# Linear attention on one core: two of its seven pairwise levels multiplied in narrow column pieces

## The chip, the cores and the metric

The kernel runs on one NeuronCore of a Trainium2 chip. The metric is the device time of one execution in microseconds (us). Engines are named as in the profile: PE is the matmul engine and PEld its weight loads, DVE, ACT and POOL are the vector, scalar and general engines, SP issues most DMAs.

## The reference

One layer of a decoder step in float32: a prompt of 2048 tokens and 8 single decode tokens, width 1024. After a norm and one projection, half of the heads do sliding-window attention (window 128) and half do gated linear attention (4 heads, keys of 64, values of 128). Then come an output projection and a SwiGLU block of width 2816. The part that the change touches is the linear attention:

```python
def gla_chunked(q, k, v, log_a, s0):   # S_t = diag(a_t) S_{t-1} + k_t^T v_t, o_t = q_t S_t
    b = jnp.cumsum(ac, axis=2)
    o_inter = jnp.einsum('nhtd,nhdv->nhtv', qc * jnp.exp(b), S)
    decay = jnp.exp(jnp.where(causal, b[t] - b[s], -inf))
    scores = jnp.einsum('nhtd,nhsd,nhtsd->nhts', qc, kc, decay)
    o = o_inter + jnp.einsum('nhts,nhsv->nhtv', scores, vc)
```

## The kernel before

The program has three stages: projection and window attention (to about 427 us), linear attention (about 427 to 720 us), and the output projection with the SwiGLU block (the rest, a Strassen scheme of F32R matmuls). It is written with the Tile framework. The last lines of the file build it with `schedule_with_timeline_sim=True`: a scheduler orders each engine's instructions when the program is built, by dependencies and by durations that it estimates. What an engine runs is therefore not the order of the source, and work of neighbouring loop passes is interleaved.

The linear attention takes two chunks of 128 tokens at a time: `gla_b(pp)` for pp = 0 to 7, with `front_b(pp + 1)` (projections of the next pair, tiles `ps_qk`, `ps_v`, `ps_g`) after each. Inside `gla_b` the scores of a chunk are put together from seven levels, H = 64, 32, 16, 8, 4, 2, 1 (line 53 names them `LEVELS`). At level H a chunk falls into blocks of 2H tokens, and the queries of the upper half of each block meet the keys of its lower half. For each level:

- DVE forms differences of cumulated gates (`E`, L799), ACT takes the absolute value and the exponential (L800, L801).
- POOL writes decayed queries into one of three `bd` tiles (L813, two instructions); `bd[:, :, g]` holds two heads' 64 queries each, 128 columns. DVE multiplies the keys into `E` (L814).
- PE multiplies `E` and `bd` in float32 for the four pairs g = 2a + c of head pair a and chunk c (L817 and L818). All 128 tokens of a chunk stand as weights, so all 128 partitions of `ps_l` are written, though only the 64 lower-half tokens are wanted. The profile shows each float32 matmul as two records, hence 8 records a level.
- For H = 64 and 32 ACT copies the wanted rows out of PSUM into the score tile `AT` (L820 to L824, one copy and two copies). For the five smaller levels DVE copies under a mask (L828).

`ps_l` has two PSUM banks (pool `b_lv`). When all levels are done, `AT` is multiplied with the values (`po`, L867) and the state is updated: `pst` (L875) is a float32 matmul with 64 weight columns, whose results lie in partitions 0 to 63 and 64 to 127 in turn. Other float32 matmuls of the block are `ps_d` (L836), with two moving columns.

Of the kernel before, what the change touches and what calls it, by code (L numbers as in the profile page):

```python
# [20 lines left out]
P = 128  # L21
# [30 lines left out]
def hymba_kernel(ctx: ExitStack, tc: tile.TileContext, I, O, X=None, phases=3):  # L52
    nc = tc.nc
# [538 lines left out]
    with ExitStack() as ph:  # L592
# [69 lines left out]
        for i in range(2):  # L662
            AT = pc.tile([P, 4, 2, P], F32, name=f"AT{i}")
# [7 lines left out]
        for i in range(3):  # L671
            bd = bdp.tile([P, 2, 4, 64], F32, name=f"bd{i}")
# [98 lines left out]
        def split_wo(i, behind):  # L771


            if raw_wo:
                wr, dh, k0 = raw_wo.pop()
                hl = wop.tile([P, 2, 2, 512], F32R, tag="hl", name="wohl")
                with tc.issue_after(behind.ins):
                    split(hl[:, 0], hl[:, 1], wr.rearrange("p (k n) -> p k n", k=2))
                nc.sync.dma_start(wo_d[dh][:, :, k0:k0 + 2], hl.bitcast(F32))
            if i < 8:  # L780
                dh, k0 = i // 4, 2 * (i % 4)
                wr = wop.tile([P, 1024], F32, tag="wr", name="wro")
                for dst, src in load_wo(wr, k0, dh):
                    nc.sync.dma_start(dst, src)
                raw_wo.append((wr, dh, k0))

        def gla_b(pp):
            qT, kTt, Bt, vs, rs = live.pop(pp)

            AT = ATs[pp % 2]  # L790
            q2 = qT[:, :, 0:256].rearrange("p a (c t) -> p a c t", c=2)
            k2 = kTt[:, :, 0:256]
            for li, H in enumerate(LEVELS):
                J = 64 // H

                E = wl.tile([P, 2, 256], F32, tag="E", name="E", bufs=4)
                Bv = Bt.rearrange("p a (n t) -> p (a n) t", t=2 * H)
                Ev = E.rearrange("p a (n t) -> p (a n) t", t=2 * H)
                nc.vector.tensor_tensor(Ev, Bv, Bv[:, :, H - 1:H].to_broadcast([P, 4 * J, 2 * H]), ALU.subtract)  # L799
                nc.scalar.activation(E, E, AF.Abs)  # L800
                grown = nc.scalar.activation(E, E, AF.Exp, scale=-1.0 / 16)  # L801

                if li in (1, 5) and 2 <= 2 * pp + li // 5 <= 10:
                    split_wo(2 * pp + li // 5 - 2, grown)
                bd = bds[nbd[0] % 3]
                nbd[0] += 1
                qv = qT[:, :, 0:256].rearrange("p a (n two o) -> p a n two o", two=2, o=H)
                kv = kTt[:, :, 0:256].rearrange("p a (n two o) -> p a n two o", two=2, o=H)
                E5 = E.rearrange("p a (n two o) -> p a n two o", two=2, o=H)
                bv = bd.rearrange("p h (a c) (j o) -> p h a (c j) o", a=2, o=H)  # L810
                for h in range(2):
                    rows = slice(64 * h, 64 * h + 64)
                    nc.gpsimd.tensor_tensor(bv[rows, h], E5[rows, :, :, 1], qv[rows, :, :, 1], ALU.mult)  # L813
                nc.vector.tensor_tensor(E5[:, :, :, 0], E5[:, :, :, 0], kv[:, :, :, 0], ALU.mult)  # L814
                ps = lvp.tile([P, 512], F32, tag="lv", name="ps_l")
                Ef = E.rearrange("p a t -> p (a t)")
                for g in range(4):  # L817
                    nc.tensor.matmul(ps[:, g * P:(g + 1) * P], Ef[:, g * P:(g + 1) * P],  # L818
                                     bd[:, :, g], start=True, stop=True)
                if H >= 32:  # L820
                    for j in range(J):
                        rows = slice(2 * H * j, 2 * H * j + H)
                        nc.scalar.copy(AT[rows].rearrange("p g h t -> p (g h) t")[:, :, 2 * H * j + H:2 * H * j + 2 * H],
                                       ps[rows].rearrange("p (g t) -> p g t", t=64)[:, :, H * j:H * j + H])  # L824
                else:
                    av = AT.rearrange("p g h (j two o) -> p (g h) j two o", two=2, o=H)[:, :, :, 1]
                    mk = lmask[:, li * 64:(li + 1) * 64].rearrange("p (j o) -> p j o", o=H).unsqueeze(1)
                    nc.vector.copy_predicated(av, mk.to_broadcast([P, 8, J, H]),  # L828
                                              ps.rearrange("p (g j o) -> p g j o", g=8, o=H))
# [3 lines left out]
            ps = aux.tile([P, 512], F32, tag="aux", name="ps_d")  # L833
# [17 lines left out]
            ps = aux.tile([P, 512], F32, tag="aux", name="ps_kd")  # L851
# [5 lines left out]
            for c in range(2):  # L857
# [4 lines left out]
                for p in range(2):  # L862
                    g = 2 * p + c
                    last = p == 1
                    for h in range(2):
                        hc = slice((2 * p + h) * P, (2 * p + h + 1) * P)
                        nc.tensor.matmul(po[:, hc], AT[:, g, h, :], v[:, hc], start=(p == 0 and h == 0),  # L867
                                         stop=(last and h == 1 and b == 0), skip_group_check=True)
                    if b > 0:
                        nc.tensor.matmul(po[:, p * 256:(p + 1) * 256], eBf[:, g * P:(g + 1) * P], Sbd[:, p, :],  # L870
                                         start=False, stop=last, skip_group_check=True)

                    for h in range(2):
                        rows = slice(64 * h, 64 * h + 64)
                        nc.tensor.matmul(pst[rows, p * P:(p + 1) * P], kdN[:, g, rows], v[:, (2 * p + h) * P:(2 * p + h + 1) * P],  # L875
                                         start=True, stop=True)
                for p in range(2):
                    g = 2 * p + c
                    for h in range(2):
                        rows = slice(64 * h, 64 * h + 64)  # L880
# [3 lines left out]
                for hh in range(4):  # L884
                    p, h = hh // 2, hh % 2
# [13 lines left out]
                ps = aux.tile([P, 512], F32, tag="aux", name="ps_m")  # L899
# [57 lines left out]
        for pp in range(NB // 2):  # L957
            gla_b(pp)
            next(dec, None)
            if pp + 1 < NB // 2:  # L960
                front_b(pp + 1)
# [487 lines left out]
```

## Time and profile before

| what | value |
|---|---|
| runs, median (lowest to highest of 3) | 2265.45 us (2263.92 to 2266.01) |
| the profiled execution, its own time | 2265.43 us |
| span of that execution | 2263.7 us |
| granted PE clock, mean | 0.989 |
| matmul records of L818 | 448 |
| copies of L823 | 24 |

The profiled execution's time is its span and 1.7 us around it. Busy time and shares are counted inside the span. A matmul record's duration includes the pipeline behind it, so the rate of a group is read from the starts of its neighbours.

### The profile page before, as it was taken

The page shows a single profiled execution, that of the slowest core. Times are in us where ns is not written, and L with a number is a line of the kernel's source. Part 1 is how long each engine was busy: PE and PEld are TensorE (multiplying, and loading weights), DVE is VectorE, ACT ScalarE, POOL GpSimd, SP SyncE. Part 2 cuts the span into 40 slices and gives each one's busy share as a digit, 9 for nine tenths or more (in the row PEclk, how much of TensorE's full clock was granted, in tenths as well). Part 3 has the DMA queues.
Part 4 walks back from the last instruction along what each step waited for, and adds up shares of the span by engine and source line. Part 5 has one row for each costly group of instructions (what it writes and reads, how often), then busy time and mean ns, then how long its engine had stood idle before and what let it go on. Part 6 is the DMA issues. An engine that isn't in the chain of part 4 may idle for free.

```text
span 2263.7 us, 34888 instructions
## 1 busy us (share of the span) xinstructions
PE 2201.3 (97%) x12697; PEld 1903.6 (84%) x12697; DVE 1566.6 (69%) x3076; ACT 1006.7 (44%) x2259; POOL 624.7 (28%) x706
## 2 busy tenths in 40 slices
PE   8999998999998999999999999999999899999997
PEld 6888887888887788688888889999999878787886
DVE  6787888677765667776667666676766665757487
ACT  6766777465654334433323233333333334434342
POOL 2443434465664233211111111110111122222222
PEclk9999999999999999999999999999999999999999
DMA  7323334445515998933333375233332477878776
GB/s 235 119 75 108 111 106 159 116 150 172 168 49 217 330 317 275 350 112 95 110 98 94 116 253 203 85 117 89 103 99 87 148 195 176 202 168 230 166 209 233
DMA packets 211992, 364.75 MB, mean 161 GB/s; under 512 B 15683, under 2 KB 129116, under 8 KB 208732
## 3 DMA queue, kind: packets, MB, share of 16 engines
q1 hardware_dynamic: 174764, 259.05, 34.9%
q0 software_dynamic: 37056, 103.47, 18.0%
q8 instruction: 100, 1.64, 0.3%
q14 instruction: 72, 0.59, 0.1%
HBM read 211.24 MB, written 152.29 MB: 161 GB/s over the span
## 4 chain that ended last, share of the span: by engine, by line
PE 69%; issue 17%; POOL 6%; DVE 4%; DMA 2%; ACT 1%; SPq 0%; POOLq 0%; DVEq 0%; ACTq 0%
PE ps_b L108 6%; PE ps_b L107 6%; PE ps_b L109 6%; PE ps_c L108 4%; PE ps_c L107 4%; PE ps_c L109 4%; POOL h_d L1380 4%; PE ps_a L108 4%; PE ps_a L107 4%; PE ps_a L109 4%; PE ps_d L107 3%; PE ps_d L109 3%; PE ps_d L108 3%; PE ps_wo L107 2%; PE ps_wo L109 2%
## 5 line engine op out<-in xcount | busy, mean ns | idle before, releaser
L109 PE MATMUL ps_b<-z,whl 128*128 128x258 f32 (+1 forms) x792 | 253.4, 320 | 2.1 <-DVE whl L96 2.1
L107 PE MATMUL ps_b<-z,whl 128*128 128x258 f32 (+1 forms) x792 | 254.1, 321 | 1.2 <-ACT whl L95 1.2
L108 PE MATMUL ps_b<-z,whl 128*128 128x258 f32 (+1 forms) x792 | 254.3, 321 | 0.0
L95 ACT CAST dm<-mr 128x384 fp32r<-128x384 f32 (+1 forms) x224 | 108.3, 488 | 188.3 <-PE ps_b L109 100.8
L108 PE MATMUL ps_a<-z,whl 128*128 128x258 f32 (+1 forms) x528 | 169.2, 320 | 0.0
L108 PE MATMUL ps_c<-z,whl 128*128 128x258 f32 (+1 forms) x528 | 169.1, 320 | 0.0
L109 PE MATMUL ps_a<-z,whl 128*128 128x258 f32 (+1 forms) x528 | 168.9, 320 | 0.0
L109 PE MATMUL ps_c<-z,whl 128*128 128x258 f32 (+1 forms) x528 | 168.9, 320 | 0.0
L107 PE MATMUL ps_a<-z,whl 128*128 128x258 f32 (+1 forms) x528 | 168.8, 320 | 0.0
L107 PE MATMUL ps_c<-z,whl 128*128 128x258 f32 (+1 forms) x528 | 168.6, 319 | 0.0
L109 PEld LDWEIGHTS ps_b<-z,whl 128*128 128x128 f32 x792 | 149.5, 189 | 14.6 <-DVE whl L96 2.5
L107 PEld LDWEIGHTS ps_b<-z,whl 128*128 128x128 f32 x792 | 149.6, 189 | 13.2 <-ACT whl L95 1.3
L108 PEld LDWEIGHTS ps_b<-z,whl 128*128 128x128 f32 x792 | 149.4, 189 | 12.0
L96 DVE TENSOR_TENSOR dm<-mr,dm 128x384 fp32r<-128x384 f32 (+1 forms) x224 | 115.4, 519 | 59.3 <-ACT dm L95 59.3
L95 ACT CAST whl<-wrg 128x512 fp32r<-128x512 f32 x132 | 81.6, 619 | 155.0 <-PE ps_b L109 81.0
L985 DVE TENSOR_TENSOR gu<-ps_c,gu 128x512 f32<-128x512 f32 (+1 forms) x130 | 78.0, 600 | 58.2 <-PE ps_c L109 57.6
L96 DVE TENSOR_TENSOR whl<-wrg,whl 128x512 fp32r<-128x512 f32 x132 | 90.8, 689 | 36.6 <-ACT whl L95 36.3
L1284 POOL DMA_DIRECT2D md_d<-m x22 | 15.7, 713 | 363.5 <-DVE m L1247 363.5
L813 POOL TENSOR_TENSOR bd<-E,qTb 64x256 f32<-64x256 f32 x112 | 102.5, 915 | 44.8 <-ACT E L801 35.1
L95 ACT CAST whl<-sy 128x512 fp32r<-128x512 f32 x88 | 54.5, 620 | 131.9 <-PE ps_b L109 84.4
L107 PEld LDWEIGHTS ps_c<-z,whl 128*128 128x128 f32 x528 | 99.8, 189 | 8.2 <-issue 0.3
L107 PEld LDWEIGHTS ps_a<-z,whl 128*128 128x128 f32 x528 | 99.7, 189 | 8.0
(399 smaller groups left out, 6668.0 us busy)
## 6 DMA issues: line engine op xcount, KB each, us to landing
mr<-md_d SPq DMA_DIRECT2D x24, 1344.0 KB, 7.7
zc_d_P<-zhl POOLq DMA_DIRECT2D x56, 512.0 KB, 6.5
z<-zc_d_P SPq DMA_DIRECT2D x14, 2048.0 KB, 28.9
wrg<-in_w_gate_dram SPq DMA_DIRECT2D x44, 512.0 KB, 5.8
wrg<-in_w_up_dram SPq DMA_DIRECT2D x44, 512.0 KB, 4.0
nT_d<-nT SPq DMA_DIRECT2D x16, 1024.0 KB, 5.3
zT<-nT_d SPq DMA_DIRECT2D x8, 2048.0 KB
h_d<-gu POOLq DMA_DIRECT2D x48, 256.0 KB, 4.6
```

Of the source, the lines that this page charges most:

```text
L95: nc.scalar.copy(h, src)
L96: (eng or nc.vector).tensor_tensor(l, src, h.bitcast(F32), ALU.subtract)
L107: nc.tensor.matmul(ps, lh, rh, start=start, stop=False, skip_group_check=more)
L108: nc.tensor.matmul(ps, lh, rl, start=False, stop=False, skip_group_check=more)
L109: nc.tensor.matmul(ps, ll, rh, start=False, stop=stop, skip_group_check=more)
L813: nc.gpsimd.tensor_tensor(bv[rows, h], E5[rows, :, :, 1], qv[rows, :, :, 1], ALU.mult)
L985: nc.vector.tensor_tensor(out, a, b, ALU.add)
L1284: nc.gpsimd.dma_start(md_d[sb][g][:, :, q, fp - GROUPS[g][0], :], src.rearrange("p (m t) -> p m t", m=4))
L1380: nc.gpsimd.dma_start(h_d[ti][:, cols], c, accum_op=ALU.add)
```

## The change

Only the two largest levels change. Their matmuls take as weights just the H lower-half tokens of each block (64 columns, or twice 32), and as moving operand just the H queries of that block in both heads (128 columns, or 64). Each piece writes its own 64 or 32 partitions of `ps_l`; the chunk c and the block j choose which. Level 64 has 4 matmuls, as before; level 32 has 8 instead of 4. ACT copies each partition group alone: two copies at level 64, four at level 32. The five smaller levels keep their code in the other branch.

```diff
-                for g in range(4):
-                    nc.tensor.matmul(ps[:, g * P:(g + 1) * P], Ef[:, g * P:(g + 1) * P],
-                                     bd[:, :, g], start=True, stop=True)
                 if H >= 32:
-                    for j in range(J):
-                        rows = slice(2 * H * j, 2 * H * j + H)
-                        nc.scalar.copy(AT[rows].rearrange("p g h t -> p (g h) t")[:, :, 2 * H * j + H:2 * H * j + 2 * H],
-                                       ps[rows].rearrange("p (g t) -> p g t", t=64)[:, :, H * j:H * j + H])
+
+                    for a in range(2):
+                        for c in range(2):
+                            for j in range(J):
+                                first = a * 256 + c * P + 2 * H * j
+                                nc.tensor.matmul(ps[64 * c + H * j:64 * c + H * j + H, a * 2 * H:(a + 1) * 2 * H],
+                                                 Ef[:, first:first + H], bd[:, :, 2 * a + c, H * j:H * j + H],
+                                                 start=True, stop=True)
+                    for c in range(2):
+                        for j in range(J):
+                            src = slice(64 * c + H * j, 64 * c + H * j + H)
+                            nc.scalar.copy(AT[2 * H * j:2 * H * j + H, c::2, :, 2 * H * j + H:2 * H * j + 2 * H],
+                                           ps[src, 0:4 * H].rearrange("p (a h t) -> p a h t", a=2, h=2))
                 else:
+                    for g in range(4):
+                        nc.tensor.matmul(ps[:, g * P:(g + 1) * P], Ef[:, g * P:(g + 1) * P],
+                                         bd[:, :, g], start=True, stop=True)
```

## Rows read from the trace of the kernel before

**Rows 1.** The page, busy time by engine over the whole span.

```profile
span 2263.7 us, 34888 instructions
PE 2201.3 (97%) x12697; PEld 1903.6 (84%) x12697; DVE 1566.6 (69%) x3076; ACT 1006.7 (44%) x2259; POOL 624.7 (28%) x706
```

**Rows 2.** Windows: stretch; its length, busy us (instructions) by engine, clock, DMA.

```profile
core 0: us, PE busy (x) PEld busy (x) DVE busy (x) ACT busy (x) POOL busy (x), PEclk, DMA share, GB/s
427.00:720.00 293.00, 277.95 (x1913) 245.53 (x1913) 208.19 (x371) 174.58 (x441) 173.72 (x164) 0.98 0.43 147
```

**Rows 3.** One line's view, L818: the level matmuls and what they waited for.

```profile
L818 PE MATMUL ps_l<-bd,E x448: 270/275/582, 427.3 to 706.4; 128*128 128x128 f32 x150
its engine sat idle before it (us, times) until:
  POOL bd L813: 12.3, 17
  issue: 4.7, 8
  DVE AT L828: 2.7, 3
```

**Rows 4.** Timeline of PE around one level: start us, us, line, shapes.

```profile
501.42 0.28 PE L108 MATMUL ps_qk<-zT,W 128*128 128x256 f32 x1
501.54 0.28 PE L109 MATMUL ps_qk<-zT,W 128*128 128x256 f32 x1
501.66 1.05 PE L818 MATMUL ps_l<-bd,E 128*128 128x128 f32 x8
502.47 0.36 PE L107 MATMUL ps_qk<-zT,WQ 128*128 128x256 f32 x1
```

**Rows 5.** Timeline of PE and PEld around the 64-column matmuls of `pst`.

```profile
518.55 0.28 PE L107 MATMUL ps_qk<-zT,WQ 128*128 128x256 f32 x1
518.76 0.66 PE L875 MATMUL pst<-v,kdN 128*64 128x128 f32 x8
519.35 0.39 PE L108 MATMUL ps_qk<-zT,WQ 128*128 128x256 f32 x1
...
519.35 0.19 PEld L108 LDWEIGHTS ps_qk<-zT,WQ 128*128 128x128 f32 x1 [0.17 <-issue]
```

**Rows 6.** Timeline of PE, the matmuls with two moving columns.

```profile
628.94 0.95 PE L836 MATMUL ps_d<-hsel,qk 128*128 128x2 f32 x8
629.75 0.36 PE L107 MATMUL ps_qk<-zT,W 128*128 128x256 f32 x1
```

**Rows 7.** Groups by shape, ACT: copies out of PSUM: busy us, mean ns.

```profile
L823 ACT COPY AT<-ps_l 32x256 f32<-32x256 f32 x16 | 5.7, 357 | 0.6 <-PE ps_l L818 0.5
L704 ACT COPY kTb<-ps_qk 128x256 f32<-128x256 f32 x13 | 4.8, 368 | 15.6 <-PE ps_qk L109 15.6
L823 ACT COPY AT<-ps_l 64x512 f32<-64x512 f32 x8 | 4.6, 574 | 1.4 <-PE ps_l L818 1.4
...
L95 ACT CAST lrT<-ps_k 16x128 fp32r<-16x128 f32 x14 | 3.5, 250 | 3.7 <-DVE kT L327 3.6
```

**Rows 8.** One line's view, L823: whom the ACT copies kept waiting (none listed).

```profile
its engine sat idle before it (us, times) until:
  PE ps_l L818: 1.9, 6
who waited for it (us, times):
busy tenths in 40 slices 0000000000000000000000000000000000000000
```

**Rows 9.** Timeline of PE in the last pass of `gla_b`.

```profile
691.46 2.30 PE L818 MATMUL ps_l<-bd,E 128*128 128x128 f32 x16
698.94 0.48 PE L902 MATMUL ps_m<-ident,r 128*128 128x128 f32 x1 [5.17 <-ACT r L898]
...
701.45 5.20 PE L818 MATMUL ps_l<-bd,E 128*128 128x128 f32 x24
```

**Rows 10.** Windows, the stretch of those 24 records (columns as in rows 2).

```profile
701.40:706.40 5.00, 5.00 (x26) 5.00 (x25) 2.32 (x3) 1.99 (x3) 3.97 (x4) 0.50 1.03 412
```

## The prediction

> **What bounds it now.** I read the page's busy times first: PE is busy for 97% of the span, ACT for 44% [rows 1]. So work on PE is the first suspect for time, and ACT has room on average. The change touches one stage only, so I then asked for the busy times of that stretch: from 427 to 720 us PE is busy for 277.95 of 293.00 us, ACT for 174.58 [rows 2]. PE bounds the stage, but not everywhere: about 15 us of it are idle, and the view of the level matmuls says what ended idle time before them: POOL's writing of `bd` (12.3 us in 17 places), the issue (4.7 us), and DVE's masked copies, which free the PSUM banks (2.7 us) [rows 3]. ACT's copies are not among these. So a level's matmuls cost their full length where PE has other work queued, and less or nothing where PE would wait for POOL or for ACT's exponentials anyway.
>
> **What one level costs now.** Starts of neighbours give the price. Plain `ps_qk` records start 0.12 us apart (501.42, 501.54). The eight records of a level start 0.12 us after the last of these, and the next `ps_qk` record starts 0.81 us later (501.66 to 502.47) [rows 4]. A level therefore takes 0.81 us of PE. Two levels in eight passes are changed, 16 of the 56; that is 16 x 0.81 = 13.0 us of PE, the most that could be won if they cost nothing.
>
> **Level 64: four matmuls of 64 weight columns.** These have an exact counterpart in the trace: `pst` has 128 rows, 64 weight columns, 128 moving columns, in float32, and alternates between the lower and the upper 64 partitions, as the new code does with c. Its eight records last 0.66 us from the first start to the last end. With about 0.27 us for one record (the shortest of the full ones is 0.270 [rows 3]) the starts are (0.66 - 0.27) / 7 = 0.055 us apart, half of the full array's (1.05 - 0.275) / 7 = 0.11 [rows 4, 5]. But the group starts 0.21 us after the `ps_qk` record ahead of it where 0.12 is normal, and the next `ps_qk` starts 0.59 us later, where 8 x 0.055 = 0.44 would do; PEld shows 0.17 us of waiting for issue there [rows 5]. The price of the whole group is 0.09 + 0.59 = 0.68 us: 0.44 us of records and 0.24 us for going into the narrow form and back. Against 0.81 us that is 0.13 us less, and 8 x 0.13 = 1.0 us less in all. The other end: if each pair were cut off from the next by other work, the 0.24 us would be paid twice, 0.92 us, or 0.9 us more in all.
>
> **Level 32: eight matmuls of 32 weight columns and 64 moving columns.** They make 16 records instead of 8. No row shows a quarter of the array. The lower end is a pace that halves again with half the columns, 0.028 us: 16 x 0.028 + 0.24 = 0.69 us, or 0.12 us less a level, 1.0 us less in all. If the pace stays at that of `pst`, 0.055 us, a level takes 0.88 + 0.24 = 1.12 us, 2.5 us more in all. The far upper end is the pace of `ps_d`, whose eight records have two moving columns and still start (0.95 - 0.25) / 7 = 0.10 us apart [rows 6], so that they are held by the weight load or the issue and not by the columns: 16 x 0.10 + 0.24 = 1.84 us, 8.2 us more in all. The nearest row is `pst`, which has narrow weights too and differs in size by a factor of two. I take the middle between its pace and half of it, 0.042 us: 0.67 + 0.24 = 0.91 us, 0.10 us more than now, 0.8 us more in all.
>
> **The copies.** Now ACT does one copy of 64x512 and two of 32x256, 0.574 + 2 x 0.357 = 1.29 us a pass [rows 7]. Afterwards there are two of 64x256 and four of 32x128. By the 256-element rows (0.357 and 0.368 us) the first cost 0.36 us each; by the 16x128 cast out of PSUM the others cost 0.25 us each [rows 7]. Together 1.72 us, 0.43 us more a pass and 3.5 us more of ACT in all, in 24 more instructions. I cost this at nothing: nothing is listed as waiting for the copies [rows 8], `AT` is read only after five more levels, and ACT is idle for 118 of the stage's 293 us [rows 2]. What can bite is ACT's queue: behind a copy stand the exponentials of later levels, for which POOL's `bd` and then PE wait. If that cover is gone everywhere, it is 3.5 us more. Both new copies and matmuls use a `ps_l` bank; the bank comes free at most 0.43 us later at level 32, and PE's waits for a bank are now all for DVE's copies [rows 3].
>
> Here a rule speaks against the change. The Trainium skill, TensorEngine Tiling (Array Packing), section PSUM Bottleneck, says that tiling speeds up TensorE but not the emptying of PSUM, so that the copies can become the limit. By that rule all 3.5 us would be on the path, and the sum would be 2268.7 us; by rows 8 it is 2265.2 us. I go by the rows.
>
> **The sum.** -1.0 + 0.8 + 0 = -0.2 us, on the profiled execution's own time of 2265.43 us: 2265.2 us. That execution lies at the median of the runs shown (2265.45), so no correction is due. A difference of 0.2% (4.5 us) is about what a measurement of this kernel can tell from none, and every step above is smaller. If PE does win time, it is POOL's `bd` that is late next, as it already is in 17 places.
>
> **Rivals.**
>
> *Slow quarters.* The 32-column pieces do not overlap, and each record is held as `ps_d` is, at 0.10 us. Its place is the eight level-32 groups; its price is +8.2 us against -1.0 us at level 64: 2272.6 us, slower than before. With the gain at level 64 the two break even at a pace of 0.044 us, and slower by over 4.5 us begins at 0.079 us, where 8 x (16 x 0.079 + 0.24 - 0.81) - 1.0 = 4.6. For it: `ps_d` shows that moving fewer columns need not help. Against it: `ps_d` loads full weights, and the rows of `pst`, with half the weight columns, run at half the pace. Chance 0.10.
>
> *Full overlap without a changeover.* All pieces run side by side, level 64 takes half of 0.81 us and level 32 a quarter: 8 x (0.405 + 0.61) = 8.1 us less, 2257.3 us. For it: the pace of `pst` did halve. Against it: 0.24 us of changeover around that same group [rows 5], and PE's idle places, which would swallow part. Chance 0.06. The Trainium skill, same page, section Theoretical Speedup, gives just these factors as the most that can be had, up to 2 for 64 and up to 4 for 32; the trace agrees on the factor of the pace for 64 and shows nothing for 32.
>
> *Another order.* The instructions are ordered when the program is built, from estimated lengths, and the change alters the number and length of 16 groups on PE and ACT. The last pass shows what an order can cost: PE stands idle for 5.17 us before `ps_m` at 698.94, and the 24 level records after it take 5.20 us at a granted clock of 0.50, the 1.2 GHz level, where three levels at 0.81 us need 2.4 us [rows 4, 9, 10]. An order in which the last pass has filling work wins up to 5.2 + 2.8 = 8.0 us: 2257.2 us. One with a second such place loses as much: 2273.2 us. For it: the pause exists, and it lies in the pass in which no projections of a next pass are left to fill in. Against it: the pause hangs on ACT's `r`, behind POOL and DVE, which the change does not touch. Chance 0.14 for the gain and 0.08 for the loss.
>
> **How the numbers follow.** The forecast that the terms cancel has 0.62; its own range goes from 2263.4 us (-1.0 and -1.0) to 2270.4 us (-1.0 at level 64, +2.5 at level 32, the copies' 3.5 in full). The whole range reaches down over the two faster rivals, which lie at 2257.2 and 2257.3 us, to 2257.0, and up to 2272.0; it leaves out the two slower rivals at their full price, 0.18. Faster by over 0.2% (below 2260.9 us) has the two faster rivals and a little of the forecast's edge, 0.21; slower by over 0.2% (above 2270.0 us) the two slower ones, 0.18 and 0.01 of the edge; the rest, 0.60, lies within 0.2%.
>
> **What would show it.** The level-64 groups should be 8 records of 64 weight columns with about 0.055 us between starts and 0.68 us from neighbour to neighbour; the level-32 groups 16 records with 0.03 to 0.055 us between starts; L818 and its sister line together 448 + 64 = 512 records. ACT's copies should be 48, taking about 13.8 us instead of 10.3, and still have nobody waiting for them. PE's busy time between 427 and 720 us should move by less than 3 us. The prediction is wrong if the 32-column records start 0.08 us or more apart, if waits for the copies appear, or if the 5.17 us pause of the last pass goes or doubles: then the order, and not the pieces, made the time.

## The result, and the profile after

The changed kernel takes 2271.51 us (median; 2267.80 to 2274.74), the kernel before in the same session 2265.25 us: a ratio of 1.0031 with a 95% interval of 1.0024 to 1.0038, slower by 6.3 us between these medians. The prediction was no change (2265.2 us); the new time lies inside its range, but near the upper end, and on the side that had a chance of 0.19. The profiled execution of the changed kernel took 2270.73 us, 5.3 us more than that of the kernel before.

I read the pages first. The page of the changed kernel answers to [rows 1]:

```profile
span 2267.9 us, 35055 instructions
PE 2200.1 (97%) x12761; PEld 1895.3 (84%) x12761; DVE 1569.7 (69%) x3076; ACT 1009.6 (45%) x2283; POOL 626.2 (28%) x706
```

PE does 1.2 us less work (2201.3 to 2200.1), yet the span is 4.2 us longer. So the kernel is not slower because of added work; PE waits more. The windows of the changed kernel, with the columns of [rows 2], say the same of the stage:

```profile
427.00:720.00 293.00, 274.12 (x1935) 235.10 (x1936) 211.78 (x366) 175.45 (x457) 174.44 (x161) 0.98 0.42 144
```

PE's busy time in this stretch fell by 3.8 us (277.95 to 274.12), and its idle time rose from 15.1 to 18.9 us. In a stretch of fixed length one is the other side of the other: this shows that PE waits 3.8 us more, not what the pieces save.

**The pieces themselves.** The timeline of PE around one level of 64 and one of 32, with the columns of [rows 4]:

```profile
535.93 0.28 PE L109 MATMUL ps_qk<-zT,W 128*128 128x256 f32 x1
536.14 0.66 PE L823 MATMUL ps_l<-bd,E 128*64 128x128 f32 x8
536.73 0.39 PE L107 MATMUL ps_qk<-zT,W 128*128 128x256 f32 x1
...
538.84 0.28 PE L109 MATMUL ps_qk<-zT,WQ 128*128 128x256 f32 x1
539.05 0.43 PE L823 MATMUL ps_l<-bd,E 128*32 128x64 f32 x16
539.41 0.39 PE L107 MATMUL ps_qk<-zT,W 128*128 128x256 f32 x1
```

Both groups start 0.21 us after the record ahead of them, 0.09 us more than plain records need. The next record follows 0.59 us later at level 64 and 0.36 us later at level 32. Their prices are 0.68 and 0.45 us, against 0.81 us for a level before [rows 4]. If every pass were like this one, it would be 8 x (0.13 + 0.36) = 3.9 us of PE. That is an estimate: the fourth to seventh pass have these same starts, while in the others the groups run into each other, are cut by other work, or wait. The change does what it says; what it saved did not make the kernel faster.

The view of the tile `ps_l` in the changed kernel, all engines, answers to [rows 3]:

```profile
L833 PE MATMUL ps_l<-bd,E x320: 270/275/583, 431.9 to 707.8; 128*128 128x128 f32 x160
...
L823 PE MATMUL ps_l<-bd,E x192: 219/243/324, 425.9 to 694.6; 128*32 128x64 f32 x128, 128*64 128x128 f32 x64
...
  POOL bd L813: 17.6, 23
```

There are 320 + 192 = 512 records, as there should be, and the waits for POOL's `bd` have grown from 12.3 us in 17 places [rows 3] to 17.6 us in 23. The copies, in the groups by shape and in the view of their line, answer to [rows 7] and [rows 8]:

```profile
L829 ACT COPY AT<-ps_l 32x128 f32<-32x128 f32 x32 | 8.2, 255 | 0.4
L829 ACT COPY AT<-ps_l 64x256 f32<-64x256 f32 x16 | 5.8, 364 | 1.6 <-PE ps_l L823 1.5
```

```profile
who waited for it (us, times):
busy tenths in 40 slices 0000000000000000000000000000000000000000
```

They take 14.0 us instead of 10.3, and still nobody is listed as waiting for them.

**Where the time was lost.** A mark that occurs once a pass shows it: ACT's copy `kdN`. The timeline of ACT, third, fifth and eighth pass of the kernel before:

```profile
515.34 0.59 ACT L855 COPY kdN<-ps_kd 128x512 f32<-128x512 f32 x1 [0.66 <-PE ps_kd L853]
...
594.36 0.59 ACT L855 COPY kdN<-ps_kd 128x512 f32<-128x512 f32 x1 [0.66 <-PE ps_kd L853]
...
707.12 0.59 ACT L855 COPY kdN<-ps_kd 128x512 f32<-128x512 f32 x1 [0.45 <-PE ps_kd L853]
```

and of the changed kernel:

```profile
511.56 0.59 ACT L864 COPY kdN<-ps_kd 128x512 f32<-128x512 f32 x1 [1.84 <-PE ps_kd L862]
...
594.46 0.59 ACT L864 COPY kdN<-ps_kd 128x512 f32<-128x512 f32 x1 [1.37 <-PE ps_kd L862]
...
712.00 0.59 ACT L864 COPY kdN<-ps_kd 128x512 f32<-128x512 f32 x1 [1.47 <-PE ps_kd L862]
```

The changed kernel is ahead by 3.8 us in the third pass, level in the fifth, and behind by 4.9 us in the eighth. Of the lead in the third pass, 1.5 us was there at the start of the stage, whose first `ps_g` matmul ran at 427.18 us before and at 425.67 us after. The rest of the lead is lost in the middle passes, and the last three add 4.8 us. There a pair of matmuls stands out: the gates of the last pair of chunks (`ps_g`, L721), one for each head pair. Both write the same PSUM bank, and ACT reads it between them. First lines from the timelines of PE, DVE, POOL and ACT of the kernel before, with the lines between them left out:

```profile
668.07 0.28 PE L721 MATMUL ps_g<-lr,w 96*128 96x256 f32 x1
672.64 0.37 PE L721 MATMUL ps_g<-lr,w 96*128 96x256 f32 x1
676.50 1.27 DVE L732 TENSOR_TENSOR_SCAN Bt<-scm,la 128x256 f32<-128x256 f32 x2
680.84 5.33 POOL L813 TENSOR_TENSOR bd<-E,qTb 64x256 f32<-64x256 f32 x6 [7.10 <-ACT E L801]
729.68 0.69 ACT L904 ACTIVATE mob<-ps_m,gg 128x512 f32<-128x512 f32 x1 [4.71 <-PE ps_m L902]
```

and then lines of the changed kernel:

```profile
670.25 0.28 PE L721 MATMUL ps_g<-lr,w 96*128 96x256 f32 x1
672.77 0.47 ACT L724 ACTIVATE Bt<-ps_g,bT 128x256 f32<-128x256 f32 x1
680.52 0.47 PE L721 MATMUL ps_g<-lr,w 96*128 96x256 f32 x1
681.03 0.47 ACT L723 ACTIVATE la<-ps_g,nbT 128x256 f32<-128x256 f32 x1 [1.29 <-PE ps_g L721]
684.80 1.27 DVE L732 TENSOR_TENSOR_SCAN Bt<-scm,la 128x256 f32<-128x256 f32 x2
689.76 1.55 POOL L813 TENSOR_TENSOR bd<-E,qTb 64x256 f32<-64x256 f32 x2 [3.47 <-ACT E L801]
693.08 0.66 PE L823 MATMUL ps_l<-bd,E 128*64 128x128 f32 x8 [1.47 <-DVE E L814]
694.43 0.43 PE L823 MATMUL ps_l<-bd,E 128*32 128x64 f32 x16 [0.69 <-DVE ebl L851]
696.52 2.00 PE L833 MATMUL ps_l<-bd,E 128*128 128x128 f32 x8 [1.65 <-POOL bd L813]
699.91 2.08 PE L833 MATMUL ps_l<-bd,E 128*128 128x128 f32 x8 [1.40 <-POOL bd L813]
734.59 0.69 ACT L913 ACTIVATE mob<-ps_m,gg 128x512 f32<-128x512 f32 x1 [4.42 <-PE ps_m L911]
```

ACT had read the first gate by 673.24 us (672.77 + 0.47). The second gate matmul could then have run (in an experiment below that moves it forward it runs at 675.84), but the program had put value projections and the closing matmuls of the pass ahead of it in PE's queue: it ran at 680.52, with no wait of its own. ACT, the scan (DVE's running sum over the gates), and the first `bd` of the last pass follow it one by one, 8.3 us (scan) and 8.9 us (`bd`) later than before. The first level of the last pass begins at 693.08 us, when the projections that could have filled PE's waits were over (the last `ps_v` starts at 691.14), and PE stands idle four times in a row, for 5.2 us together. The 5.17 us pause of the kernel before [rows 9] is gone; its length is back in pieces. The last output of the stage (`mob`) starts 4.9 us later; the whole span is 4.2 us longer. These readings point at the late gate, but they do not measure what it costs, since a mark is not the same point of the work in two orders: between the last pair's first gate and the last `mob` PE runs 79 records of the next stage's `ps_wo` in the changed kernel and 66 in the kernel before.

So there were two theories. **Order:** the pieces are worth nothing that can be measured, and the order in which the program queues its instructions decides. **Pieces:** the narrow groups or the copies themselves cost time, and the order only shows it.

### The profile page after: what moved, and what is told of

Same layout as the page of the kernel before. It is cut to its first block, busy times and chain, and to the rows that moved or that the text cites. A ratio compares the mean times of both kernels' runs of the same rounds, so it can differ in the third digit from the quotient of the medians.

```text
span 2267.9 us, 35055 instructions
## 1 busy us (share of the span) xinstructions
PE 2200.1 (97%) x12761; PEld 1895.3 (84%) x12761; DVE 1569.7 (69%) x3076; ACT 1009.6 (45%) x2283; POOL 626.2 (28%) x706
## 4 chain that ended last, share of the span: by engine, by line
PE 51%; issue 16%; POOL 6%; DVE 2%; DMA 1%; ACT 1%; SPq 0%; POOLq 0%; DVEq 0%; ACTq 0%
PE ps_b L108 6%; PE ps_b L107 6%; PE ps_b L109 6%; PE ps_c L108 4%; PE ps_c L107 4%; PE ps_c L109 4%; PE ps_a L108 4%; POOL h_d L1389 4%; PE ps_a L107 4%; PE ps_a L109 4%; PE ps_wo L107 3%; PE ps_wo L109 3%; PE ps_wo L108 3%; POOL bd L813 1%; POOL out_y_prompt_dram L1384 1%
## 5 line engine op out<-in xcount | busy, mean ns | idle before, releaser
L107 PE MATMUL ps_a<-z,whl 128*128 128x258 f32 (+1 forms) x528 | 168.8, 320 | 0.0
L107 PE MATMUL ps_wo<-WO,mt 128*128 128x512 f32 x256 | 102.9, 402 | 5.3 <-ACT mt L95 5.3
```

What stands on the lines that cost most here:

```text
L107: nc.tensor.matmul(ps, lh, rh, start=start, stop=False, skip_group_check=more)
```

## The experiments

None of these kernels leaves any of the computation out.

**Swapping order and pieces.** Every engine's instructions were chained to the order of another kernel by edges that fix the order of issue and add no wait; a group of narrow pieces stands where its full group stood, and copies likewise. One kernel has the pieces in the order of before, the other the full matmuls and the old copies in the order of after.

```diff
+    for row in order.values():
+        row = [i for k in row for i in at[k]]
+        for a, b in zip(row, row[1:]):
+            tc.add_manual_dep(b, a.name, mybir.DependencyInfo(mybir.DependencyClass.NoSync, mybir.DependencyReason.DATA),
+                              reason="pin")
```

Pieces in the order of before:

> The narrow pieces and the piecewise copies of the change, with every engine's instructions queued in the order of the kernel before (a piece stands where its full matmul stood). Theory, the order costs the time: the pieces save 0.13 us a level at 64 and 0.36 us at 32, at most 8 x 0.49 = 3.9 us, so between 2261.3 and 2265.3 us. Rival, the pieces or the copies themselves cost it: about 2271 us, as the changed kernel.

Full matmuls in the order of after:

> The full matmuls and three copies of the kernel before, queued in the order of the changed kernel. Theory, the order costs the time: no faster than the changed kernel, 2271 to 2275 us. Rival, the pieces or the copies cost it: about 2265 us, as the kernel before.

Measured: the pieces in the order of before take 2263.01 us against 2264.26, a ratio of 0.9997 (0.9989 to 1.0006): no change. The full matmuls in the order of after take 2269.03 us, 1.0021 (1.0011 to 1.0030): most of the loss is there without a single narrow piece, though it is less than the 2271 to 2275 us that were expected. In the timeline of ACT of this second kernel the last `mob` is late as well:

```profile
737.06 0.69 ACT L914 ACTIVATE mob<-ps_m,gg 128x512 f32<-128x512 f32 x1 [4.41 <-PE ps_m L912]
```

This execution took 2273.63 us, the longest of the nine of its kernel, so the late `mob` alone says little. From the stage's first gate matmul to the last `mob` it takes 309.5 us, the changed kernel 308.9 us, and the kernel before 302.5 us.

What follows: the order alone makes a loss of 0.21%. With the pieces the changed order has 0.31%, with intervals that overlap, so the times do not settle whether the pieces add to the loss there; in the order of before they add nothing.

**Moving one matmul forward.** The value projections of a pair, all but the first four steps of its first chunk, are made to stand behind the second gate matmul, in the last pair alone (first kernel) or in every pair but the first (second kernel).

```diff
-                    nc.tensor.matmul(ps[:, :W], w3[:, p * P:(p + 1) * P], lr3[:, :W], start=True, stop=True)
+                    gate = nc.tensor.matmul(ps[:, :W], w3[:, p * P:(p + 1) * P], lr3[:, :W], start=True, stop=True)
...
+                            with tc.issue_after(gate.ins) if PINNED(pp) and (c0 > 0 or k >= 4) else nullcontext():
```

In the last pair alone:

> The changed kernel with one edit to the order: in the last pair's projections the later value matmuls are queued behind the second gate matmul, which then stands 14 places behind the first instead of 28. Theory, the last pass starts late because its gates come late: 3 to 6 us less than the changed kernel, 2265 to 2268 us. Rival, the loss is spread over all passes: within 2 us of the changed kernel, 2270 to 2273 us.

In every pair but the first:

> The same edit for every pair but the first. If the late second gate matmul costs time in the middle passes too, 1 to 3 us less than with the last pair alone, 2263 to 2266 us; if only the last pass feels it, the same as with the last pair alone within 1.5 us.

Measured: 2262.20 us, 0.9988 (0.9979 to 0.9997), and 2261.24 us, 0.9982 (0.9973 to 0.9991). Both are faster than the kernel before; against the changed kernel the first is 9.3 us faster by the medians, more than the 3 to 6 us that were expected. The second is within 1.5 us of the first, as expected if only the last pass feels the late gate. PE's and DVE's timelines of the first kernel:

```profile
670.31 0.28 PE L725 MATMUL ps_g<-lr,w 96*128 96x256 f32 x1
675.84 0.28 PE L725 MATMUL ps_g<-lr,w 96*128 96x256 f32 x1
679.08 1.27 DVE L736 TENSOR_TENSOR_SCAN Bt<-scm,la 128x256 f32<-128x256 f32 x2
```

The first gate is where it was in the changed kernel (670.31 against 670.25 us), the second comes 4.7 us earlier and the scan 5.7 us earlier. What follows: with this edit the whole loss is gone, and 2 us more. How much of that the place of the gate makes is not shown, because something else moved too. Between the last pair's first gate and the last `mob` only 39 records of `ps_wo` are left of the changed kernel's 79; the others stand behind the last `mob`.

**The same place, from the other side.** The changed kernel again, and two edits of the kernel before: one queues the last pair's second gate late (behind seven of the eight steps of the first chunk's value projection), one is the early-gate edit of above.

```diff
+                            if pp == 7 and c0 == 0 and k == KD - 2:
+                                tc.add_manual_dep(gate.ins, mm.ins.name, mybir.DependencyInfo(
+                                    mybir.DependencyClass.NoSync, mybir.DependencyReason.DATA), reason="late")
```

The changed kernel again:

> The changed kernel itself, beside the others of this call, to have it on the same chip. Every theory expects its 0.31% over the kernel before again, 0.24 to 0.38%.

The kernel before with its second gate late:

> The kernel before, with its full matmuls, and one edit to the order: in the last pair's projections the second gate matmul is queued behind 21 value matmuls, as in the changed kernel. Theory, the late second gate of the last pair costs the time: 3 to 6 us slower than the kernel before, 2267 to 2271 us. Rival, the pieces are needed for the loss: within 1.5 us of the kernel before.

The kernel before with the gates early:

> The kernel before, with its full matmuls, and the later value matmuls of every pair but the first queued behind the second gate matmul. In its own order the second gate stands 11 to 19 places behind the first, so the edit moves little. Theory, the pieces save up to 3.9 us where the order is mended: 2262 to 2265 us here, 1 to 4 us more than the changed kernel with the same edit (2261.2). Rival, the pieces save nothing: the same as that, 2261 us.

Measured: the changed kernel repeats at 1.0031 (1.0021 to 1.0041). With the late gate the kernel before takes 1.0016 (1.0007 to 1.0024), 3.4 us more; the early gates win it nothing, 1.0001 (0.9992 to 1.0010). PE's and DVE's timelines of the kernel before with the late gate:

```profile
665.50 0.28 PE L721 MATMUL ps_g<-lr,w 96*128 96x256 f32 x1
674.52 0.28 PE L721 MATMUL ps_g<-lr,w 96*128 96x256 f32 x1
680.40 0.69 DVE L732 TENSOR_TENSOR_SCAN Bt<-scm,la 128x256 f32<-128x256 f32 x1
```

Here the two gates stand 9.0 us apart, where the kernel before has 4.6 us and the changed one 10.3 us, and the scan comes at 680.40 instead of 676.50. This execution came into the stage 2.6 us earlier, so the windows, with the columns of [rows 2], run from the stage's first gate matmul to the last pair's first, and from there to the last `mob`. The kernel before:

```profile
427.18:668.07 240.89, 232.07 (x1641) 206.90 (x1640) 174.77 (x308) 147.05 (x366) 144.59 (x135) 0.99 0.41 134
668.07:729.68 61.61, 55.38 (x318) 46.35 (x317) 35.78 (x68) 30.92 (x85) 31.14 (x30) 0.92 0.46 178
```

and the same kernel with the late gate:

```profile
424.61:665.50 240.89, 231.16 (x1640) 205.73 (x1639) 175.01 (x308) 146.98 (x366) 144.89 (x135) 1.00 0.41 134
665.50:729.68 64.18, 58.91 (x318) 48.04 (x317) 35.65 (x68) 30.78 (x84) 31.67 (x30) 0.89 0.45 171
```

Up to the last pair's first gate both take 240.89 us. Behind it the same 318 records of PE take 2.6 us more. PE is not idle for longer there (6.2 us before, 5.3 us with the late gate); its records last longer, at a mean granted clock of 0.89 instead of 0.92. In windows of 4 us the clock is under 1.00 from 692 to 712 us with the late gate, and from 696 to 708 us before.

What follows: a late gate makes a loss with the full matmuls too, 2.6 us in these executions and 3.4 us by the medians, about half of the change's. If it costs the changed kernel as much, the other half was lost elsewhere. The kernel before already had its gates close, so the early edit had nothing to mend there. Its 2264.58 us is also what the theory of that run expected if the pieces save time (2262 to 2265 us), against 2261 us if they save none. The run cannot tell the two apart, because its order is not that of the changed kernel with early gates; the last experiment can.

**The copies alone.** The order of before, full matmuls, each old copy split in two by pairs (`SPLIT` is both levels), which gives the number and sizes of the new ones.

```diff
+                        for part in range(1 + (H in SPLIT)):
+                            gs = slice(part, None, 2) if H in SPLIT else slice(None)
+                            c_ = nc.scalar.copy(AT[rows, gs, :, 2 * H * j + H:2 * H * j + 2 * H],
+                                                ps[rows].rearrange("p (g h t) -> p g h t", h=2, t=64)[:, gs, :, H * j:H * j + H])
```

> The full matmuls of the kernel before in its own order, but the copies of the two levels split in two each, as many instructions and elements as in the changed kernel. Theory, copies are off the path: within 1 us of the kernel before. Rival, the copies in ACT's queue hold up the exponentials: up to 3.5 us more, 2265 to 2268 us.

Measured: 1.0001 (0.9992 to 1.0010). The groups by shape of this kernel on ACT:

```profile
L836 ACT COPY AT<-ps_l 32x128 f32<-32x128 f32 x32 | 6.6, 251 | 0.5 <-PE ps_l L829 0.4
L836 ACT COPY AT<-ps_l 64x256 f32<-64x256 f32 x16 | 5.0, 363 | 1.3 <-PE ps_l L829 1.3
```

The means per copy, 251 and 363 ns, are those of the changed kernel (255 and 364), but the busy time is 6.6 + 5.0 = 11.6 us, not 14.0: here copies of one group read the same partitions, and one begins before the one ahead has ended (four in 0.83 us, where the changed kernel takes 1.04). So this run tests the 24 more instructions, but only 1.3 of the 3.7 us more of ACT. The other part is in the first experiment: the pieces in the order of before have copies of 8.2 and 5.8 us, 14.0 us in all, and 0.9997. What follows: no cost of the copies can be measured, as the view with nobody waiting had said. (In the order of before, with the pieces, one masked copy of DVE waits 0.4 us for them.)

**Each level alone, with the gates early.** The early-gate kernel twice more with one level's pieces taken back, `NARROW` being the levels that keep them, and once as it was.

```diff
-                if H >= 32:
+                if H >= 32 and H not in NARROW:
+                    for g in range(4):
+                        nc.tensor.matmul(ps[:, g * P:(g + 1) * P], Ef[:, g * P:(g + 1) * P],
+                                         bd[:, :, g], start=True, stop=True)
...
+                elif H >= 32:
```

As it was:

> The changed kernel with the mended order of every pair, once more, beside its two halves. Expected: its 0.18% under the kernel before again, 0.09 to 0.27%.

Only level 32 narrow:

> The mended order, with narrow pieces at level 32 alone (level 64 as before). Level 32 took 0.45 us of PE for 0.81, so 2.9 of the 3.9 us saved on PE are its own: theory, 2 to 3 us under the kernel before. Rival, what is won is another order drawn by chance: no closer to the whole than to nothing, within 1.5 us of the kernel before.

Only level 64 narrow:

> The mended order, with narrow pieces at level 64 alone. Level 64 took 0.68 us of PE for 0.81, 1.0 us in all: theory, 0 to 1.5 us under the kernel before. Rival, another order by chance: as far from the kernel before as the kernel with both levels, or slower.

Measured: 0.9985 (0.9976 to 0.9994) as it was, but 1.0019 (1.0010 to 1.0028) with level 32 alone and 1.0013 (1.0005 to 1.0022) with level 64 alone. For level 32 neither theory nor rival had expected a loss. If pieces had a price of their own, two losses would not add up to a gain. Nor is it the gate: with level 32 alone the last pair's gates start at 668.28 and 673.60 us, with level 64 alone at 664.91 and 669.69, about as close as in the kernel before. PE's timeline of the first of the two shows other pauses in the last pass:

```profile
698.45 1.66 PE L849 MATMUL ps_l<-bd,E 128*128 128x128 f32 x8 [3.63 <-DVE AT L853]
703.11 0.48 PE L927 MATMUL ps_m<-ident,r 128*128 128x128 f32 x1 [3.00 <-ACT r L923]
```

What follows: each edit draws another order, and the gate is one place where an order can lose, not the only one. What these two lose by was not tried further. They cannot serve as a test of one level, because they change the order too.

**The full matmuls in the best order.** The last kernel pins the order of the early-gate kernel and puts the full matmuls and the old copies back into it (the same edges as in the first experiment).

> The full matmuls and three copies of the kernel before, every engine queued in the order of the changed kernel with the mended gates (a full matmul stands where its narrow pieces stood). If the mended kernel's gain over the kernel before (3 us) is the order's alone: 2261 to 2262 us. If it is the pieces' 3.9 us of PE: 2264 to 2266 us. In between, both have a part.

Measured: 2260.87 us against 2264.54, 0.9983 (0.9974 to 0.9992); with the pieces it was 0.9982 and 0.9985. This has the lowest median of the study, level with the early-gate kernel, and it has no narrow piece. The windows of the early-gate kernel with the pieces, with the columns of [rows 2], and its view of `ps_l`:

```profile
427.00:690.00 263.00, 251.77 (x1864) 218.67 (x1863) 195.83 (x346) 169.65 (x438) 165.62 (x154) 1.00 0.42 136
```

```profile
  POOL bd L818: 10.3, 16
```

and those of the same order with full matmuls:

```profile
427.00:690.00 263.00, 255.88 (x1794) 227.04 (x1792) 193.60 (x345) 164.81 (x413) 164.19 (x152) 0.99 0.41 133
```

```profile
  POOL bd L820: 4.6, 13
```

With the pieces PE works 4.1 us less in these 263 us, and over the stage its levels wait 5.7 us more for POOL's `bd`. In this order part of what PE saves goes there: it comes to the next level sooner and waits for the queries that POOL has not yet written. The last `mob` starts at 725.15 us with the pieces and at 726.40 without. Counted from the stage's first gate matmul (426.83 and 426.10 us) it is 298.3 and 300.3 us, so 2.0 us of the saving are left at the end of the stage.

The other two pairs of one order lean the same way: 301.5 us with the pieces against 302.5 in the order of before, 308.9 against 309.5 in that of the changed kernel. That these gains are real is not shown: the changed kernel, run again, differs from itself by 1.7 us here (307.2 us), and the times of the whole kernel show none. Nor is it the same wait in every order. With the pieces in the order of before, the levels wait less for `bd` (9.8 us against 12.3), and longer for the issue (7.7 against 4.7) and for DVE's `AT` (5.3 against 2.7). In the order of the changed kernel the wait for `bd` is 17.6 us with the pieces and 16.3 us without.

All orders and forms in one table (ratio to the kernel before; the two forms of a row have the same order):

| order | full matmuls | narrow pieces |
|---|---|---|
| of the kernel before | 1 | 0.9997 (0.9989 to 1.0006) |
| of the changed kernel | 1.0021 (1.0011 to 1.0030) | 1.0031 (1.0024 to 1.0038) |
| with the gates early | 0.9983 (0.9974 to 0.9992) | 0.9982 (0.9973 to 0.9991) |

Down a column the time moves by up to 0.5%, along a row by no more than 0.1%, within the intervals.

## Why the prediction was right and wrong

- **What bounds the kernel.** Right in part: PE bounds the stage on average, but the levels wait for POOL's `bd`. "If PE does win time, it is POOL's `bd` that is late next" held in the order with early gates (4.6 to 10.3 us) and a little in that of the changed kernel (16.3 to 17.6 us). In the order of before that wait fell (12.3 to 9.8 us) and others grew.
- **Level 64.** Right. Priced at 0.68 us from `pst`, measured 0.68 us.
- **Level 32.** Mis-sized: 0.91 us was taken, with 0.69 us as the lower end; it measured 0.45 us. I let the pace halve once more with half the columns, to 0.028 us, and named 0.03 to 0.055 us between starts as the sign. With the 0.24 us that a narrow record lasts by the median of both forms, the starts are (0.43 - 0.24) / 15 = 0.013 us apart, half of that again. That fits four column groups that run side by side where `pst` has two; the ends of records are modelled, so the 0.45 us of the whole group is the safer number. The Trainium skill, TensorEngine Tiling (Array Packing), section Theoretical Speedup, gives factors of up to 2 and up to 4; the pace shows them (0.11 to 0.055 to 0.013 us, with half the moving columns in the last), the level as a whole does not: 0.81 / 0.68 = 1.2 and 0.81 / 0.45 = 1.8. The rival of slow quarters fell. The sum would have been 8 x 0.36 + 1.0 = 3.9 us less, still under what can be told from none. PE's busy time from 427 to 720 us was to move by less than 3 us and moved by 3.8 us, but a stretch of fixed length shows a later kernel, too.
- **The copies.** Right: 13.8 us forecast, 14.0 us measured, nobody waiting, 1.0001 with the copies split alone, and 0.9997 with all 14.0 us of them in the order of before. The rule of the Trainium skill, TensorEngine Tiling (Array Packing), section PSUM Bottleneck, that the emptying of PSUM may become the limit, would have put 3.5 us on the path; these two runs do not bear it out here. One reading was off, and nothing hangs on it: the 0.43 us by which a bank was to come free later at level 32 is the sum of both levels; for level 32 alone the prediction's prices give 4 x 0.25 - 2 x 0.357 = 0.29 us.
- **The order.** This is the step that failed. The sum costed the new order at nothing, and the loss from it stood only as a rival with a chance of 0.08. The runs showed in its place 0.21% (about 4.8 us) from the new order alone, with the full matmuls. That the rival's 8.0 us come near the 6.3 us between the medians is luck: it was the price of a second long pause in the last pass, and no second one came. Its place was argued wrongly: "the pause hangs on ACT's `r`, behind POOL and DVE, which the change does not touch". That pause disappeared, which the prediction named as a sign of the order; the waits that came in its place follow a late gate matmul at the head of that chain, and no row that I read spoke of its place in PE's queue. Such a late gate by itself costs the kernel before 3.4 us, about half of the loss. The argument took the chain of the old order as if it were fixed. A fixed chain is what a newly drawn order does not keep.
- **The chances.** Drawing the order again moved this kernel both ways: of the seven orders that the scheduler drew in this study beside that of before, four lost (one of them by intent), two won, and one did neither; the ratios run from 0.9982 to 1.0031. With 0.22 for another order, and 0.62 for terms that cancel, I gave the smaller chance to the effect that was larger than the whole sum.

What stays open: why the scheduler, given shorter groups, put the second gate behind more value projections; what makes the last pass of the two single-level kernels lose; by which wait the first passes' lead went between the third and the fifth pass, where two executions of the changed kernel already differ (its fifth mark comes 168.8 and 167.1 us after the stage's first gate matmul); and how the kernel with one gate moved wins more than that gate costs. The order theory is shown for the change as a whole; a late gate of the last pair is shown, in the kernel before, as a place that costs about half as much, and where the rest is lost is not shown.

## What to carry to other kernels

Where a scheduler orders the instructions when the program is built, an edit is two changes: the work, and a new order of everything around it. Price the second by its own spread, and pin the order when the work of an edit is to be measured. Compare marks in two traces only where the order of the work is the same. And before making matmuls shorter, look at what their groups wait for: PE time saved ahead of a wait is given back in it, at least in part (here 4.1 us saved, 2.0 us left, in the order with early gates).

## What the runs showed of the hardware

- Narrow float32 matmuls into four different column ranges run nearly side by side: 16 records in a group of 0.36 + 0.09 us, against 0.81 us for 8 full ones.
- A group of them pays a changeover that does not shrink with the pieces: 0.24 us beside `pst` [rows 5], 0.24 us of the 0.68 us here at level 64, and 0.45 - 16 x 0.013 = 0.24 us at level 32. The Trainium skill, TensorEngine Tiling (Array Packing), section Key Properties, says that a change of the tiling mode drains TensorE; the 0.09 us ahead of either group and the slower start behind it are in line with that, while the drain itself is in no row. So a short group wins much less than its factor.
- Copies out of PSUM that read the same partitions overlapped by a little in ACT's records (four of 32x128 in 0.83 us), copies from four different partition groups did not (1.04 us).
- In the last pass PE's time was not set by the length of its waits alone. With the late gate they were short ones (1.73, 0.93 and 1.27 us ahead of levels between 690 and 699 us), where the kernel before has one of 5.17 us [rows 9]; PE was idle for 5.3 us instead of 6.2 us, yet the same 318 records were busy for 58.9 us instead of 55.4 us. The mean granted clock was 0.89 instead of 0.92, and 0.5 from 692 to 700 us, the 1.2 GHz level.
